# Rows of inverse norms by a ones-times-diagonal product, and state products in halves of 256 columns

## The chip, the cores and the metric

The kernel runs on one core of a Trainium2 chip. The metric is the device time of one execution in microseconds. Three runs of the kernel before took 3521.5, 3522.03 and 3524.02 us; their median, 3522.03 us, is the number to be changed. A measurement of this kernel can tell about 0.2% (7 us) from no change.

## What is computed

One layer of a hybrid model on 256 tokens behind 16 meta tokens (272 rows, width 2048, float32):

1. `n = rmsnorm(h)`, and one input projection `n @ w_in` for everything that follows.
2. A retention mixer with 8 heads: rotary on q and k, scores with a decay mask, values of 512 channels a head, then an RMS norm of each token over the 512 channels of its head, `o = _rms(o)`, times `silu(g)`, and an output projection of 4096 x 2048.
3. A state-space mixer with 8 groups of 8 heads of 64 channels: a causal convolution of width 4, a chunked scan over two chunks of 128 tokens (products within a chunk, and a state carried between chunks), times `silu(z)`, an RMS norm of each token over the 512 channels of its group, and a projection of 4096 x 2048.
4. Both mixers gated and added, projected, added to `h`; then an RMS norm over 2048 channels, a product-key selection of 16 of 16384 experts for each of 8 heads, and the experts' two layers (all 16384 rows of `peer_u` and `peer_v` are streamed), a last residual and norm.

There are thus 17 norms whose inverse must stand as a row over tokens, the same on every partition: 8 heads, 8 groups, and the norm ahead of the experts. Channels lie on the partitions and tokens along the free axis, so the sum over channels is a sum over partitions, and its result has to reach all partitions again.

## The kernel before

`Stream` (L35) fixes the order of all work. TensorE's main work is a queue of 2244 weight pieces of [128, 512]. Every piece is loaded by SyncE (L89, two pieces in one transfer of 512 KB), split on ScalarE into a rounded part `wh` (L99) and on VectorE into the rest `wl` (L100), and used by 12 float32r products (L202 to L204, four contraction tiles with three products each). The splits are written two pieces ahead of the products (`LEAD = 2`) and go through four buffers; loads are written six pieces ahead. All engines run their instructions strictly in the order in which they are written.

Everything else is written between the pieces by generators: `yield 3` means that the next step is written three pieces later, at the earliest; further numbers in a yield are microseconds of VectorE and ScalarE work, and such a step is put off to a later piece while credit for that engine is used up. So the order of instructions is fixed when the program is built and does not depend on times.

The retention part runs head after head, 48 pieces each (`ret_head`, steps `attend`, `gtile`, `gated`). Then come the retention's output projection, 8 state-space groups of 40 pieces (`ssm_group`, steps `btile`, `ctile`, `mats`, `xtile`, `scan`, `ztile`, `gated`), the second output projection (`mixer_out`, first 20 pieces of gates, then products that need the 32 tiles `Q.gh`/`Q.gl`), the residual (`resid`), the queries (`query`, `topk`), and the experts.

A norm is made by `norm_col` (L165): two products with a column of ones put the sums of 256 tokens into two PSUM columns (L169), one piece later VectorE (L162) and GpSimd (L163, a power of -0.5) make the inverse root `ncol`, 128 x 2. `to_rows` (L175) then writes it to DRAM with a transfer of 256 single elements (L178) and reads it back to all 128 partitions with a second (L179), both on GpSimd's queue; the second waits for the first in GpSimd's own order.

Who uses the row `r`: in `gated` of a head, VectorE's L367 (sg times r), then L369, ScalarE's L371 and VectorE's L373. In `gated` of a group, GpSimd's L699 (y times r, four pieces after the transfers are written), then ScalarE's L704 (gh) and VectorE's L708 (gl). In the residual, `Q.rb`, used by the experts.

In the state-space part GpSimd also carries, in this order between one group's norm and the next: `meta` (L610, a copy of the leading tokens), L620, the two products m times cb (L587), L638, transfers L597 and L554, L558, y times z (L687), and the sums of squares L691 and L692. The `meta` copy is what TensorE's L622 transposes, in the middle of the stream of pieces.

The two state products of `scan` (L631 and L633) are float32 products of 512 columns:

```python
z1 = P.pso.tile([128, 512], F32, name="sc")
pe.matmul(z1, bk0, x0.rearrange("p e s c -> p (e s c)"), start=True, stop=True)
z2 = P.pso.tile([128, 512], F32, name="tp", bufs=2)
pe.matmul(z2, bk, x1.rearrange("p h e -> p (h e)"), start=True, stop=True)
```

Of the kernel before, what the change touches and what calls it, by code (L numbers as in the profile page):

```python
# [34 lines left out]
class Stream:  # L35
    """The tensor engine's main work in order: weight pieces of [128, 512], each split into two float32r
    parts ahead of its products. Other work runs between the pieces, as generators. They yield the number of
    pieces to wait for and, where it is worth counting, how long the next step holds VectorE and ScalarE, in
    microseconds: a step that isn't urgent waits for a piece with time to spare."""
# [38 lines left out]
    def need(self, ready):  # L78
        """Emits the pending other work early until ready()."""
        while not ready():  # L80
            _, patient, _, gen, _ = heapq.heappop(self.side)
            self.step(gen, not patient, 0)
# [44 lines left out]
def build(ctx, tc, a):  # L127
# [32 lines left out]
    def rsqrt(dst, ps, mul, add):  # L160
        """dst = (mul * ps + add) ** -0.5"""
# [3 lines left out]
    def norm_col(w, psp, name, sq, mul, add):  # L165
        """Sums over the partitions of sq [128, S], as (mul * sum + add) ** -0.5 in [token, block]."""
# [6 lines left out]
        return c  # L173

    def to_rows(dst, c):  # L175
        """dst[p, t] for every partition p from [token, block]"""
        d = P.dram.tile([2, 128], F32, name="rows", bufs=4)
        pool.dma_start(d.rearrange("b t -> t b"), c)  # L178
        pool.dma_start(dst, bass.AP(tensor=d.tensor, offset=d.offset, ap=[[0, 128], [1, S]]))  # L179
# [5 lines left out]
    def product(srcs, moving, done, hook=None, count=None):  # L185
        """One output tile [128, n]: pieces of 4 contraction tiles, three float32r products for each.
        done(psum) is a generator with the rest; count() tells how many tiles of the moving operand are there."""
# [35 lines left out]
    # ------------------------------------------------------------ retention  # L223
    def ret_head(h):
# [76 lines left out]
        def attend():  # L301
# [43 lines left out]
            c = yield from norm_col(w, P.pso, "s0", sq[:, 0], 4.0 / 512, 4.0 * EPS)  # L345
            B["r"] = r = w.tile([128, S], F32, name="r")
            to_rows(r, c)
# [43 lines left out]
    # ------------------------------------------------------------ the mixers' output projections  # L391
# [37 lines left out]
    # ------------------------------------------------------------ state space  # L429
# [101 lines left out]
    def bc(x, n):  # L531
        """[p, 8] as [p, 8, n]"""
        return x.unsqueeze(2).to_broadcast([x.shape[0], 8, n])

    def ssm_group(g):
# [69 lines left out]
        def scan():  # L605
# [25 lines left out]
            pe.matmul(z1, bk0, x0.rearrange("p e s c -> p (e s c)"), start=True, stop=True)  # L631
            z2 = P.pso.tile([128, 512], F32, name="tp", bufs=2)
            pe.matmul(z2, bk, x1.rearrange("p h e -> p (h e)"), start=True, stop=True)  # L633
# [50 lines left out]
        def gated():  # L684
# [9 lines left out]
            c = yield from norm_col(P.ssm, P.pso, "s0", z[:, 0], 1.0 / 512, 4.0 * EPS)  # L694
            r = P.ssm.tile([128, S], F32, name="r")
            to_rows(r, c)
            yield 4
# [27 lines left out]
    # ------------------------------------------------------------ residual, expert queries  # L725
# [14 lines left out]
    def resid(j):  # L740
        def done(p):
# [16 lines left out]
            if j == NK - 1:  # L758
                yield 2
                Q.rt = yield from norm_col(P.bconst, P.psm, "mix", Q.ssq, 1.0 / D, EPS)  # L760
                to_rows(Q.rb, Q.rt)
                st.spawn(topk(), 1)
# [52 lines left out]
    def topk():  # L815
# [4 lines left out]
        def picked(b, h, pos, ixf):  # L820
            """The two key numbers of each of the 16 chosen pairs."""
# [66 lines left out]
    # ------------------------------------------------------------ experts  # L888
# [12 lines left out]
    def zblk(i, j, t0, t1):  # L901
        """Z[:, i:j, t0:t1] in at most two views with their start"""
# [150 lines left out]
    # ------------------------------------------------------------ the program  # L1053
# [211 lines left out]
```

## Time and profile before

| what | value |
|---|---|
| median of three runs | 3522.03 us |
| span of the profiled execution, first to last instruction | 3535.0 us |
| time of the profiled execution beside that span | not given by the page; the span alone is 13.0 us over the median |
| TensorE busy | 97% of the span |
| VectorE, ScalarE, GpSimd busy | 67%, 49%, 19% |
| mean granted TensorE clock | 0.984 |

A float32 product stands in the trace as two instructions (two passes), a float32r product as one. "Busy" counts an instruction from its start to its modelled end, and products overlap, so the sum over a line can be larger than the time that it takes; the idle time before an instruction, in brackets with what ended it, is the number used below. A piece of 256 columns takes 1.42 us, one of 272 columns 1.52 us.

### The profile page before, as it was taken

What the parts mean: (1) busy time and instruction counts of PE and PEld (TensorE: products, weight loads), DVE (VectorE), ACT (ScalarE), POOL (GpSimd) and SP (SyncE); (2) the same over time, 40 slices, a digit from 0 to 9 for tenths busy, and PEclk for the clock granted to TensorE, in tenths of its full rate; (3) what the DMA queues carried; (4) which work ended last, traced back from release to release, by engine and by line L of the source; (5) the groups of instructions that cost most, each with busy time, mean ns of one, the idle gap of its engine ahead of it and who ended that gap; (6) DMA issues with size and microseconds to landing.
All of it is one profiled execution on the core that took longest, in us unless ns stands there. A gap on an engine that the chain in (4) does not pass through costs nothing.

```text
span 3535.0 us, 66214 instructions
## 1 busy us (share of the span) xinstructions
PE 3414.0 (97%) x25242; PEld 3259.7 (92%) x25242; DVE 2352.7 (67%) x4550; ACT 1732.7 (49%) x3131; POOL 675.8 (19%) x784
## 2 busy tenths in 40 slices
PE   9999999999999998898999999999999999999999
PEld 8999989999998888888999999999999988888887
DVE  7555455555576776775556789989999755555555
ACT  5444444444454444444444555555555554555555
POOL 2111111100012222321002111156678500000000
PEclk9999999999999999999999999999999999999999
DMA  5566665566556565555556755655555566666665
GB/s 184 156 149 148 160 158 147 152 195 195 185 171 163 157 158 157 151 157 152 185 185 215 205 180 186 186 178 174 175 178 174 180 197 200 192 192 196 193 194 184
DMA packets 177613, 622.39 MB, mean 176 GB/s; under 512 B 21200, under 2 KB 27216, under 8 KB 177040
## 3 DMA queue, kind: packets, MB, share of 16 engines
q1 hardware_dynamic: 172288, 603.20, 58.0%
q0 software_dynamic: 5008, 14.96, 1.6%
q8 instruction: 198, 3.24, 0.4%
q14 instruction: 119, 0.97, 0.1%
HBM read 613.75 MB, written 4.34 MB: 175 GB/s over the span
## 4 chain that ended last, share of the span: by engine, by line
PE 86%; DMA 6%; issue 4%; POOL 2%; DVE 1%; ACT 1%; DVEq 0%; POOLq 0%; SPq 0%; ACTq 0%
PE acc L202 21%; PE acc L204 21%; PE acc L203 21%; PE y L1001 7%; PE y L1003 7%; PE y L1002 7%; DMA rows<-ncol 4%; DMA r<-rows 2%; PE g L933 1%; DVE wl L100 1%; POOL y L699 1%; PE yd L664 0%; POOL y L687 0%; POOL ncol L163 0%; PE sc L268 0%
## 5 line engine op out<-in xcount | busy, mean ns | idle before, releaser
L100 DVE TENSOR_TENSOR wl<-raw,wh 128x512 fp32r<-128x512 f32 x2244 | 1631.8, 731 | 1061.9 <-ACT wh L99 1043.4
L99 ACT ACTIVATE wh<-raw 128x512 fp32r<-128x512 f32 x2244 | 1407.1, 630 | 1341.2 <-PE acc L203 918.9
L204 PE MATMUL acc<-xh,wl 128*128 128x256 f32 (+1 forms) x3216 | 930.8, 289 | 38.3 <-DVE wl L100 38.1
L202 PE MATMUL acc<-xh,wh 128*128 128x256 f32 (+1 forms) x3216 | 943.3, 293 | 3.1 <-ACT wh L99 3.1
L203 PE MATMUL acc<-xl,wh 128*128 128x256 f32 (+1 forms) x3216 | 926.8, 288 | 0.0
L204 PEld LDWEIGHTS acc<-xh,wl 128*128 128x128 f32 x3216 | 620.2, 193 | 42.3 <-DVE wl L100 42.1
L204 PE MATMUL acc<-xgh,wl 128*128 128x256 f32 x2304 | 644.4, 280 | 0.0
L202 PE MATMUL acc<-xgh,wh 128*128 128x256 f32 x2304 | 643.9, 279 | 0.0
L203 PE MATMUL acc<-xgl,wh 128*128 128x256 f32 x2304 | 643.9, 279 | 0.0
L202 PEld LDWEIGHTS acc<-xh,wh 128*128 128x128 f32 x3216 | 621.1, 193 | 10.4 <-ACT wh L99 4.9
L203 PEld LDWEIGHTS acc<-xl,wh 128*128 128x128 f32 x3216 | 619.1, 193 | 1.9 <-issue 1.9
L203 PEld LDWEIGHTS acc<-xgl,wh 128*128 128x128 f32 x2304 | 432.8, 188 | 0.0
L204 PEld LDWEIGHTS acc<-xgh,wl 128*128 128x128 f32 x2304 | 432.5, 188 | 0.0
L202 PEld LDWEIGHTS acc<-xgh,wh 128*128 128x128 f32 x2304 | 432.3, 188 | 0.0
L1001 PE MATMUL y<-wh,wzh 128*128 128x512 f32 x1024 | 400.2, 391 | 0.0
L1003 PE MATMUL y<-wh,wzl 128*128 128x512 f32 x1024 | 398.7, 389 | 0.0
L1002 PE MATMUL y<-wl,wzh 128*128 128x512 f32 x1024 | 398.6, 389 | 0.0
L202 PE MATMUL acc<-gh,wh 128*128 128x256 f32 (+1 forms) x1152 | 330.2, 287 | 13.5 <-ACT wh L99 13.5
L203 PE MATMUL acc<-gl,wh 128*128 128x256 f32 (+1 forms) x1152 | 331.2, 288 | 2.0 <-DVE gl L708 1.9
L204 PE MATMUL acc<-gh,wl 128*128 128x256 f32 (+1 forms) x1152 | 330.0, 286 | 1.4 <-DVE wl L100 1.4
L202 PEld LDWEIGHTS acc<-gh,wh 128*128 128x128 f32 x1152 | 223.3, 194 | 14.1 <-ACT wh L99 13.7
L1003 PEld LDWEIGHTS y<-wh,wzl 128*128 128x128 f32 x1024 | 192.2, 188 | 40.2
(292 smaller groups left out, 3629.0 us busy)
## 6 DMA issues: line engine op xcount, KB each, us to landing
raw<-in_win SPq DMA_DIRECT2D x418, 512.0 KB, 3.6
raw<-in_pu SPq DMA_DIRECT2D x256, 512.0 KB, 3.5
raw<-in_pv SPq DMA_DIRECT2D x256, 512.0 KB, 3.5
raw<-in_wro SPq DMA_DIRECT2D x64, 512.0 KB, 3.5
raw<-in_wso SPq DMA_DIRECT2D x64, 512.0 KB, 3.5
raw<-in_wout SPq DMA_DIRECT2D x32, 512.0 KB, 4.0
raw<-in_wq SPq DMA_DIRECT2D x32, 512.0 KB, 3.7
m<-acs_d POOLq DMA_DIRECT2D x16, 512.0 KB, 7.1
```

The lines of the kernel that those rows point to most:

```text
L99: self.nc.scalar.activation(h, r, AF.Copy)
L100: self.nc.vector.tensor_sub(lo, r, h.bitcast(F32))
L202: pe.matmul(p, h[:, s], mh[:, kk], start=kk == 0, stop=False)
L203: pe.matmul(p, h[:, s], ml[:, kk], start=False, stop=False)
L204: pe.matmul(p, lo[:, s], mh[:, kk], start=False, stop=kk == nk - 1)
L699: pool.tensor_mul(y, y, r.unsqueeze(1).to_broadcast([128, 4, S]))
L933: pe.matmul(ps[:, t % NB].rearrange("p a b -> p (a b)"), o[:, 0], o[:, 1:].rearrange("p a b -> p (a b)"), start=True, stop=True)
L1001: pe.matmul(y, wh[:, s], h, start=i == 0, stop=False)
L1002: pe.matmul(y, wh[:, s], lo, start=False, stop=False)
L1003: pe.matmul(y, wl[:, s], h, start=False, stop=i == NE - 1)
```

## The change

A generator `norm_rows` takes the place of `norm_col` and `to_rows`. After the inverse root, GpSimd multiplies the identity with it: `diag`, 128 x 256, holds two diagonal matrices side by side. Three pieces later TensorE multiplies ones (128 x 128) with `diag`; the result, in the upper half of the PSUM tile that held the sums, is the row on every partition. One piece after that the generator returns. The heads use the row from PSUM; the groups and the residual copy it to SBUF on ScalarE. In the groups, the y times r step is then written one piece later than before. The two state products become four, of 256 columns each.

```diff
-    def norm_col(w, psp, name, sq, mul, add):
+    def norm_rows(w, psp, name, sq, diag, mul, add):
         ps = psp.tile([128, 512], F32, name=name)
         for b in range(2):
             pe.matmul(ps[:, b:b + 1], sq[:, b * 128:b * 128 + 128], ones[:, :1], start=True, stop=True)
         yield 1
         c = w.tile([128, 2], F32, name="ncol", bufs=2)
         rsqrt(c, ps[:, :2], mul, add)
-        return c
-
-    def to_rows(dst, c):
-        d = P.dram.tile([2, 128], F32, name="rows", bufs=4)
-        pool.dma_start(d.rearrange("b t -> t b"), c)
-        pool.dma_start(dst, bass.AP(tensor=d.tensor, offset=d.offset, ap=[[0, 128], [1, S]]))
+        pool.tensor_tensor(diag.rearrange("p (b t) -> p b t", b=2), ident.unsqueeze(1).to_broadcast([128, 2, 128]),
+                           c.unsqueeze(2).to_broadcast([128, 2, 128]), op=OP.mult)
+        yield 3
+        pe.matmul(ps[:, S:], ones, diag, start=True, stop=True)
+        yield 1
+        return c, ps[:, S:]
...
-            c = yield from norm_col(w, P.pso, "s0", sq[:, 0], 4.0 / 512, 4.0 * EPS)
-            B["r"] = r = w.tile([128, S], F32, name="r")
-            to_rows(r, c)
+            _, B["r"] = yield from norm_rows(w, P.pso, "s0", sq[:, 0], sq[:, 1], 4.0 / 512, 4.0 * EPS)
...
-            pe.matmul(z1, bk0, x0.rearrange("p e s c -> p (e s c)"), start=True, stop=True)
+            for i in (0, 256):
+                pe.matmul(z1[:, i:i + 256], bk0, x0.rearrange("p e s c -> p (e s c)")[:, i:i + 256],
+                          start=True, stop=True)
...
-            pe.matmul(z2, bk, x1.rearrange("p h e -> p (h e)"), start=True, stop=True)
+            for i in (0, 256):
+                pe.matmul(z2[:, i:i + 256], bk, x1.rearrange("p h e -> p (h e)")[:, i:i + 256],
+                          start=True, stop=True)
...
-            c = yield from norm_col(P.ssm, P.pso, "s0", z[:, 0], 1.0 / 512, 4.0 * EPS)
+            _, rp = yield from norm_rows(P.ssm, P.pso, "s0", z[:, 0], z[:, 1], 1.0 / 512, 4.0 * EPS)
             r = P.ssm.tile([128, S], F32, name="r")
-            to_rows(r, c)
-            yield 4
+            act.activation(r, rp, AF.Copy)
+            yield 1
...
-                Q.rt = yield from norm_col(P.bconst, P.psm, "mix", Q.ssq, 1.0 / D, EPS)
-                to_rows(Q.rb, Q.rt)
+                Q.rt, rp = yield from norm_rows(P.bconst, P.psm, "mix", Q.ssq, P.h2p.tile([128, S], F32, name="hsq", bufs=2), 1.0 / D, EPS)
+                act.activation(Q.rb, rp, AF.Copy)
```

## Rows read from the trace of the kernel before

**Rows 1.** The page: the span, the busy times of the engines, and the chain that ended last, by engine and by line (shares of the span).

```profile
span 3535.0 us, 66214 instructions
PE 3414.0 (97%) x25242; PEld 3259.7 (92%) x25242; DVE 2352.7 (67%) x4550; ACT 1732.7 (49%) x3131; POOL 675.8 (19%) x784
...
PE 86%; DMA 6%; issue 4%; POOL 2%; DVE 1%; ACT 1%; DVEq 0%; POOLq 0%; SPq 0%; ACTq 0%
```

**Rows 2.** Busy time by stage. Columns: the window's length, then busy time and (x instructions) of PE, weight loads, DVE, ACT and POOL, the granted clock, DMA share, GB/s. The stages are the heads, the first group (no norm of an earlier group falls in it), and the other groups with the start of the second output projection.

```profile
30.00:703.00 673.00, 635.28 (x4995) 626.07 (x4994) 358.92 (x588) 288.79 (x508) 76.03 (x91) 0.97 0.59 154
...
1005.00:1085.00 80.00, 79.49 (x648) 77.28 (x648) 61.20 (x121) 41.03 (x74) 17.85 (x15) 1.00 0.57 178
1085.00:1655.00 570.00, 504.36 (x3993) 486.56 (x3992) 388.20 (x706) 257.07 (x472) 145.11 (x116) 0.94 0.59 154
```

**Rows 3.** Groups of instructions by line, TensorE alone, in the window of the heads (30 to 703 us): busy time and mean, then idle time before them and what ended it.

```profile
L202 PE MATMUL acc<-xh,wh 128*128 128x256 f32 (+1 forms) x1437 | 421.4, 293 | 3.1 <-ACT wh L99 3.1
L204 PE MATMUL acc<-xh,wl 128*128 128x256 f32 (+1 forms) x1437 | 417.9, 291 | 34.3 <-DVE wl L100 34.3
```

**Rows 4.** The same view in the window of the groups and the start of the second output projection (1005 to 1655 us).

```profile
L204 PE MATMUL acc<-xh,wl 128*128 128x272 f32 (+1 forms) x1306 | 379.0, 290 | 4.0 <-DVE wl L100 3.8
L202 PE MATMUL acc<-gh,wh 128*128 128x256 f32 x54 | 16.0, 296 | 7.2 <-ACT wh L99 7.2
L203 PE MATMUL acc<-gl,wh 128*128 128x256 f32 x53 | 15.8, 298 | 1.9 <-DVE gl L708 1.9
L622 PE MATMUL tp<-ident,meta 128*64 128x128 f32 x8 | 3.2, 399 | 53.1 <-POOL meta L610 45.3 <-DVE xd L617 7.8
```

**Rows 5.** The timeline of the first head's norm: start and duration in us, engine, line, operation; in brackets the idle time before it and what ended that.

```profile
88.45 0.50 PE L169 MATMUL s<-ones,sq 128*128 128x1 f32 x4
91.06 0.94 POOL L178 DMA_DIRECT2D rows<-ncol  x1 [0.31 <-POOL ncol L163]
104.97 1.15 ACT L99 ACTIVATE wh<-raw 128x512 fp32r<-128x512 f32 x2 [5.25 <-DMA raw<-in_win]
108.43 1.23 DVE L367 TENSOR_TENSOR sg<-sg,r 128x1024 f32<-128x1024 f32 x1 [7.98 <-DMA r<-rows]
110.31 0.41 PE L204 MATMUL acc<-xh,wl 128*128 128x272 f32 x1 [4.14 <-DVE wl L100]
```

**Rows 6.** Transfers: KB of each and median us to landing; first those of the whole span, then the weights in the window 84 to 112 us.

```profile
raw<-in_win SPq DMA_DIRECT2D x418, 512.0 KB, 3.6
...
rows<-ncol POOLq DMA_DIRECT2D x17, 1.0 KB, 9.8
...
raw<-in_win SPq DMA_DIRECT2D x6, 512.0 KB, 11.0
```

**Rows 7.** The timeline around the norm of the second group, columns as in rows 5. The third row begins the last of the 16 contraction tiles of the four pieces that follow the sums; the product added by the change stands behind that tile.

```profile
1156.62 0.50 PE L169 MATMUL s<-ones,sz 128*128 128x1 f32 x4
1162.65 0.77 POOL L178 DMA_DIRECT2D rows<-ncol  x1 [0.30 <-POOL ncol L163]
1162.88 0.28 PE L202 MATMUL acc<-xh,wh 128*128 128x256 f32 x1
...
1182.13 0.23 POOL L610 COPY meta<-xs 128x64 f32<-128x64 f32 x1
1182.20 0.91 ACT L704 ACTIVATE gh<-y,gss 128x256 fp32r<-128x256 f32 x2 [8.17 <-POOL y L699]
1182.41 0.42 PE L622 MATMUL tp<-ident,meta 128*64 128x128 f32 x1 [8.20 <-POOL meta L610]
```

**Rows 8.** Busy time (columns of rows 2) in 16 windows, each from TensorE's first product after one of the 16 waits to the end of the half-clock stretch that the wait set off (clock 0.50 in 15 of them, 0.53 in the first): the sum of all.

```profile
sum 69.16, PE 67.28 PEld 66.96 DVE 51.77 ACT 44.95 POOL 9.32; mean PE 4.20 PEld 4.19 DVE 3.24 ACT 2.81 POOL 0.58
```

**Rows 9.** Starts of every third product of a piece, inside the last of these stretches and after it (timeline, TensorE).

```profile
1641.83 0.41 PE L202 MATMUL acc<-xh,wh 128*128 128x256 f32 x1
1642.47 0.41 PE L202 MATMUL acc<-xh,wh 128*128 128x256 f32 x1
...
1644.20 0.28 PE L202 MATMUL acc<-xh,wh 128*128 128x256 f32 x1
1644.56 0.28 PE L202 MATMUL acc<-xh,wh 128*128 128x256 f32 x1
```

**Rows 10.** The nearest operations to those added. First the chain in order of time (start us, us on the chain, what): L268 is four passes of 256 and four of 144 columns, L631 two passes of 512. Then groups by line: a product of 256 elements a partition with an operand spread by a zero step on GpSimd, and an activation of 256 elements out of PSUM on ScalarE.

```profile
130.74 1.35 PE sc L268 x8
1034.74 1.05 PE sc L631 x2
...
L829 POOL TENSOR_TENSOR oh<-oh,ixf 128x256 f32<-128x256 f32 x32 | 32.1, 1021 | 43.1 <-DVE oh L827 43.1
L677 ACT ACTIVATE cth<-acc 128x256 f32<-128x256 f32 x32 | 12.2, 380 | 33.6 <-PE acc L204 32.2 <-issue 1.4
```

**Rows 11.** GpSimd beside VectorE and TensorE (timeline): the m times cb products of the fifth interval, and y times z of the third.

```profile
1419.58 5.20 POOL L587 TENSOR_TENSOR m<-m,cb 128x1024 f32<-128x1024 f32 x2 [3.52 <-ACT m L584]
1422.46 2.87 DVE L100 TENSOR_TENSOR wl<-raw,wh 128x512 fp32r<-128x512 f32 x1
1425.39 0.39 PE L204 MATMUL acc<-xh,wl 128*128 128x256 f32 x1 [1.42 <-DVE wl L100]
...
1225.74 2.40 POOL L687 TENSOR_TENSOR y<-y,sz 128x1024 f32<-128x1024 f32 x1 [2.64 <-DVE y L669]
1226.61 2.08 DVE L100 TENSOR_TENSOR wl<-raw,wh 128x512 fp32r<-128x512 f32 x1 [0.95 <-ACT wh L99]
```

## The prediction

> **What bounds the kernel now.** I read the chain first, then the busy times by stage, then what TensorE waits for, line by line, and last the timeline of one wait of each kind. TensorE is busy for 97% of the 3535.0 us span, and the chain runs through it for 86%; what is left on the chain is mostly DMA, 6%, a great deal for a kernel whose weights stream ahead of their use [rows 1]. The stages show where. The first state-space group, in which no earlier norm falls, runs at full clock with TensorE idle for 80.00 - 79.49 = 0.51 us. The heads leave it idle for 673.00 - 635.28 = 37.7 us at a mean clock of 0.97, the later groups with the start of the second output projection for 570.00 - 504.36 = 65.6 us at 0.94 [rows 2]. So TensorE is the bound, and whatever it waits for in these two stages is paid in full.
>
> In the heads all of it but 0.3 us stands ahead of two lines: 34.3 us for `wl` and 3.1 us for `wh`, 37.4 us in 8 heads [rows 3]. The timeline of the first shows why: the inverse root leaves GpSimd at 91.06, its two transfers end only at 108.43, and VectorE, which is to multiply with the row, stands idle for 7.98 us with the next `wl` behind it, until TensorE has used up what was split ahead and waits 4.14 us [rows 5]. In the groups, L622 waits 53.1 us in 7 places [rows 4]: GpSimd stands in y times r until the row lands, ScalarE waits 8.17 us in gh behind it, and the small `meta` copy, which TensorE's transpose needs, is queued behind y times r; TensorE waits 8.20 us [rows 7]. At the second output projection the last group's row is late too: 7.2 us for `wh` behind a blocked gh and 1.9 us for gl [rows 4].
>
> Each wait is paid twice. After each of the 16, the granted clock stands at its lower level, 1.2 GHz: TensorE was busy for 67.3 us in such stretches [rows 8]. There three products start every 0.64 us, and 0.36 us at 2.4 GHz [rows 9], so 67.3 x (1 - 0.36/0.64) = 29.4 us were lost.
>
> **The change part by part.**
>
> *Transfers removed.* The waits worth 37.4 + 53.1 + 7.2 + 1.9 = 99.6 us end with them, and with the waits the slow stretches, 29.4 us: 129.0 us. What is late next in a head: the sums start at 88.45 and the root is ready at 91.06 [rows 5], the diagonal some 1.1 us later, at 92.2; TensorE comes to the added product after the sums (0.4 us) and four pieces of 1.42 us, at 94.5, and need not wait. VectorE reaches L367 at about 100.5, so the row has 5 us to spare. Nothing else that it needs is late, because the weight load that ScalarE awaited for 5.25 us was itself slowed while the 256 single elements were written: loads landed after 11.0 us there against a median of 3.6 [rows 5, 6].
>
> *Product added.* 17 products of ones with 256 float32 columns, two passes each. Four passes of 256 columns and four of 144 take 1.35 us [rows 10]: 0.84 ns a column, so 0.22 us a pass and 0.43 a product; 0.02 more for the change of weights gives 17 x 0.45 = 7.7 us, all on the path (from 17 x 0.3, if passes overlap with neighbours, 5 us, to 17 x 0.6, 10 us).
>
> *A new wait, TensorE for the diagonal.* TensorE runs in order, so all later pieces queue behind this product, and the two split buffers fill behind them. In a group the sums start at 1156.62 and the root is free at 1162.65; TensorE comes to the product at 1162.88 + 0.36 = 1163.24 [rows 7]. GpSimd's multiply is not in the trace; a 256-element product with a spread operand took 1.02 us [rows 10], so the diagonal stands at 1163.7 to 1163.8 and TensorE waits some 0.55 us in each of six groups: 3.3 us. The first and last groups and the residual have their root sooner. The bounds are 0 (root sooner when nothing is blocked) and 2 us in each of the 8 groups, 16 us (VectorE, which makes the root, later by another 1.5 us).
>
> *ScalarE's copy*, 9 times 0.38 us [rows 10], comes when the split that ScalarE does next still has no free buffer; I cost it at nothing. Without that cover it is 9 x 0.4 = 3.6 us.
>
> *y times r, gh and gl one piece later.* GpSimd now starts y times r some 8.5 us after the sums, so that gh could follow at 11 us; before, gh started 1182.20 - 1156.62 = 25.6 us after them [rows 7]. The `meta` copy, by the yields three pieces behind y times r, finds GpSimd free. For gh and gl every group but the last has the 40 pieces of another group as room. The last has not: its last gl was written just ahead of the piece that reads it, and now follows by one step; I count 0.7 us, between 0 and 2.
>
> *The port that VectorE and GpSimd share.* Now y times r ran while VectorE was stopped anyway; after the change it runs beside the splits, and the diagonal multiply is new. In the trace a `wl` took 2.87 us while GpSimd made m times cb for 5.20 us, and TensorE then waited 1.42 us; beside y times z another took 2.08 us and TensorE did not wait [rows 11]. All such waits in the groups are 3.8 us now [rows 4], some of them covered because TensorE had just run at half clock. Without that cover I put m times cb at 1.2 us in each of seven groups, 8.4 us, which is 5 us more than now; 0 to 20 us are possible. The Trainium skill, SBUF — State Buffer, section "SBUF: two separate sides", states that a VectorE operation with two SBUF inputs and a GpSimd operation that reads SBUF exclude each other for a whole instruction. By that rule, which speaks against this change, 17 diagonals and 8 times y times r could block VectorE for 17 x 1.0 + 8 x 2.3 = 35 us, and none of it need reach TensorE while splits lie ahead; the 2.87 us and 2.08 us above agree with it.
>
> *Halves of 256 columns.* A pass of 512 columns takes 1.05 / 2 = 0.525 us where two of 256 at the rate above take 0.43 [rows 10]. 32 such passes give 32 x 0.1 = 3.2 us. If the rate belongs to the operands and not to the width, it is 0; twice as many weight loads could cost 1 us.
>
> *The sum.* Against the profiled span: 129.0 + 3.2 - 7.7 - 3.3 - 0.7 - 5 = 115.5 us, from 3535.0 to 3419.5. The median lies 13.0 us under that span. I put these 13 us into work that stays and take the same gain off the median: 3522.0 - 115.5 = 3406.5 us.
>
> **Rivals.**
>
> *The profile's surplus lies in the waits.* If the 13.0 us by which the profiled span is longer are transfers slowed by the recording, the unrecorded kernel has less to win: 102.5 us, 3419.5. For it speaks that the experts' stage has no waits at which recording could cost time; against it, that 13 us over 16 waits of 4 to 8 us would be a large part of each.
>
> *VectorE becomes the bound in the groups.* It is busy for 61.2 of 80.0 us in the first group [rows 2], where gh and gl are still missing, and the groups get shorter. If the root comes 1.5 us later and port locks cost TensorE 3 us a group in place of 1.2, that is 8 x 1.5 + 7 x 1.8 = 25 us more: 3431. For it speaks the 6 us from sums to root [rows 7] against 2.6 in a head [rows 5].
>
> *The weight loads stay late in the heads*, because something else slows them: without the row's wait the next `wl` could still not start before 105.6, and TensorE would wait about 0.5 to 1 us in each of 8 heads, 8 us at most: 3414. Against it: 11.0 us of landing falls together with the element-wise transfer [rows 6].
>
> *Slower than before: TensorE parked behind the diagonal.* GpSimd's multiply, with both operands spread by zero steps, could take x us where I count 1.0. TensorE would then wait x - 0.6 in six groups and about x - 3.2 in the other 11 places, with a slow stretch of 29.4 / 16 = 1.8 us after each. Without any such wait the gain is 118.8 us; 17x - 38.8 + 31 reaches it at x = 7.4 us. At x = 9 the time would be 3522 + 26 = 3548. Against it stands a product with one spread operand at 1.02 us [rows 10]; no row shows two.
>
> That the change does not do what it says I see in the halves alone: 3410.
>
> **How the numbers follow.** My forecast, with its own range of 3396 to 3416 (halves and the product's price at either end, locks 0 to 10 us): 0.60. VectorE as the bound, 3431: 0.18. Surplus in the waits, 3419: 0.12. Late loads, 3414: 0.05. Parked, 3548: 0.03. A gain under 7 us by a mixture that I cannot name: 0.02. The range, 3394 to 3433, takes in the surplus, the late loads and most of the VectorE case. About 0.2%, 7 us, can be told from no change: faster 0.95, the same 0.02, slower 0.03.
>
> **What would show it.** The profile after should have no wait of more than 1.5 us in the heads, and L622 should wait for nothing. The mean clock should be near 1.00 from 30 us on. L169's successor should show some 0.5 us of waiting for the diagonal in groups 2 to 7, none in heads. Passes of 256 columns should follow each other every 0.22 us. `raw` loads should land after 3 to 5 us everywhere. I would be wrong if waits for `wl` in the groups exceeded 15 us, if the clock fell again behind waits for the diagonal, or if the diagonal's multiply took over 3 us.

## The result, and the profile after

The changed kernel takes 3401.99 us (median of four runs, 3401.59 to 3403.01) where the kernel before, with one more run beside the three, takes 3522.2 (3521.5 to 3524.02). The ratio is 0.9657, 95% interval 0.9646 to 0.9669. The gain of 120.2 us stands against 115.5 in the sum, the time against a predicted 3406.5.

The page of the changed kernel, span, busy times and chain by engine, answers to [rows 1]:

```profile
span 3400.4 us, 66296 instructions
PE 3382.4 (99%) x25308; PEld 3240.5 (95%) x25308; DVE 2359.6 (69%) x4550; ACT 1738.2 (51%) x3140; POOL 667.4 (20%) x767
...
PE 99%; DVE 0%; issue 0%; ACT 0%; DMA 0%; POOL 0%; SPq 0%; DVEq 0%; POOLq 0%
```

DMA, 6% of the chain before, is gone from it, and TensorE is busy for 99% of the span. The busy times by stage answer to [rows 2], with the same windows:

```profile
30.00:703.00 673.00, 672.75 (x5466) 666.80 (x5465) 388.94 (x631) 316.53 (x551) 70.22 (x83) 1.00 0.54 168
1005.00:1085.00 80.00, 80.00 (x668) 78.19 (x665) 63.05 (x116) 41.17 (x77) 25.26 (x20) 1.00 0.59 185
1085.00:1655.00 570.00, 570.00 (x4721) 562.06 (x4719) 424.32 (x749) 297.28 (x539) 124.84 (x96) 1.00 0.58 178
```

TensorE's idle time in the first and the third falls from 37.7 and 65.6 us to 0.25 and 0, and the clock stands at 1.00, the level of 2.4 GHz, in all three. The groups by line from 25 to 2100 us answer to [rows 3, 4]; the waits of L204 and L202 (now L205 and L203), 34.3 and 3.1 us in the heads alone, are 0.5 and 0, and the 53.1 us ahead of the transpose of `meta` (now L621) are 0. The two added products, L178, waited for nothing in all 16 heads and groups:

```profile
L203 PE MATMUL acc<-xh,wh 128*128 128x256 f32 (+1 forms) x3216 | 930.4, 289 | 0.0
L205 PE MATMUL acc<-xh,wl 128*128 128x256 f32 (+1 forms) x3216 | 915.6, 285 | 0.5 <-DVE wl L100 0.5
...
L178 PE MATMUL s<-sz,ones 128*128 128x256 f32 x16 | 4.8, 379 | 0.0
L178 PE MATMUL s<-sq,ones 128*128 128x256 f32 x16 | 4.7, 378 | 0.0
L621 PE MATMUL tp<-ident,meta 128*64 128x128 f32 x8 | 2.2, 270 | 0.0
```

Where the time came from can be read from the products of the sums, one set in each norm, which both kernels have at the same place in the order (32 instructions in 8 heads, 32 in 8 groups, 4 at the residual; durations in ns, then the first and the last start). Before:

```profile
L169 PE MATMUL s<-ones,sq x32: 164/250/251, 88.4 to 678.0; 128*128 128x1 f32 x32
L169 PE MATMUL s<-ones,sz x32: 165/250/251, 1077.7 to 1612.2; 128*128 128x1 f32 x32
L169 PE MATMUL mix<-ones,ssq x4: 167/250/251, 1975.7 to 1975.9; 128*128 128x1 f32 x4
```

After:

```profile
L171 PE MATMUL s<-ones,sq x32: 164/250/251, 88.5 to 631.0; 128*128 128x1 f32 x32
L171 PE MATMUL s<-ones,sz x32: 165/250/251, 1022.9 to 1485.4; 128*128 128x1 f32 x32
L171 PE MATMUL mix<-ones,ssq x4: 166/250/251, 1839.9 to 1840.1; 128*128 128x1 f32 x4
```

From the first head's sums to the last head's it was 589.6 us and is 542.5; from there to the first group's 399.7 and 391.9; through the groups 534.5 and 462.5; to the residual's 363.5 and 354.5; from there to the end of the span 1559.3 and 1560.5. So the heads gave 47.1 + 7.8 = 54.9 us, the groups 72.0 and the rest 9.0 - 1.2 = 7.8, together 134.7 between the two profiled executions.

The timeline around the first head's norm (start, duration, line; in brackets the idle time before it and what ended it) answers to [rows 5]:

```profile
88.49 0.50 PE L171 MATMUL s<-ones,sq 128*128 128x1 f32 x4
90.08 0.72 POOL L163 TENSOR_TENSOR ncol<-ncol,mhalf 128x2 f32<-128x2 f32 x1 [5.14 <-DVE ncol L162]
90.87 0.61 POOL L175 TENSOR_TENSOR sq<-ident,ncol 128x256 f32<-128x256 f32 x1
94.62 0.59 PE L178 MATMUL s<-sq,ones 128*128 128x256 f32 x2
100.82 1.21 DVE L366 TENSOR_TENSOR sg<-sg,s 128x1024 f32<-128x1024 f32 x1
```

The diagonal is ready at 91.48, 3.1 us before TensorE comes to it, and VectorE's product with the row starts at 100.82 instead of 108.43 and waits for nothing. Around the second group's norm, which answers to [rows 7], the diagonal is ready at 1096.48, 0.6 us before TensorE comes to it:

```profile
1090.72 0.50 PE L171 MATMUL s<-ones,sz 128*128 128x1 f32 x4
1094.49 1.10 POOL L163 TENSOR_TENSOR ncol<-ncol,mhalf 128x2 f32<-128x2 f32 x1 [4.72 <-DVE ncol L162]
1095.67 0.81 POOL L175 TENSOR_TENSOR sz<-ident,ncol 128x256 f32<-128x256 f32 x1
1097.10 0.59 PE L178 MATMUL s<-sz,ones 128*128 128x256 f32 x2
1098.19 2.42 POOL L702 TENSOR_TENSOR y<-y,r 128x1024 f32<-128x1024 f32 x1 [1.71 <-ACT r L699]
```

The weight loads in the window 84 to 112 us (KB of each, median us to landing) answer to the last line of [rows 6], 11.0 us before:

```profile
raw<-in_win SPq DMA_DIRECT2D x9, 512.0 KB, 3.8
```

### The profile page after: what moved, and what is told of

Read it like the earlier page. It is cut to its first block, busy times and chain, and to the rows that moved or that the text cites. A ratio compares the mean times of both kernels' runs of the same rounds, so it can differ in the third digit from the quotient of the medians.

```text
span 3400.4 us, 66296 instructions
## 1 busy us (share of the span) xinstructions
PE 3382.4 (99%) x25308; PEld 3240.5 (95%) x25308; DVE 2359.6 (69%) x4550; ACT 1738.2 (51%) x3140; POOL 667.4 (20%) x767
## 4 chain that ended last, share of the span: by engine, by line
PE 99%; DVE 0%; issue 0%; ACT 0%; DMA 0%; POOL 0%; SPq 0%; DVEq 0%; POOLq 0%
PE acc L203 25%; PE acc L205 25%; PE acc L204 24%; PE y L1004 7%; PE y L1006 7%; PE y L1005 7%; PE g L936 1%; PE yd L667 1%; PE sc L269 0%; PE tp L635 0%; PE sc L631 0%; PE o L333 0%; PE tp L653 0%; PE mix L798 0%; PE y L1033 0%; PE tp L651 0%
## 5 line engine op out<-in xcount | busy, mean ns | idle before, releaser
L203 PE MATMUL acc<-xh,wh 128*128 128x256 f32 (+1 forms) x3216 | 930.4, 289 | 0.0
L205 PE MATMUL acc<-xh,wl 128*128 128x256 f32 (+1 forms) x3216 | 915.6, 285 | 0.5 <-DVE wl L100 0.5
L204 PE MATMUL acc<-xl,wh 128*128 128x256 f32 (+1 forms) x3216 | 913.6, 284 | 0.0
L205 PE MATMUL acc<-xgh,wl 128*128 128x256 f32 x2304 | 645.1, 280 | 0.0
L203 PE MATMUL acc<-xgh,wh 128*128 128x256 f32 x2304 | 643.8, 279 | 0.0
L204 PE MATMUL acc<-xgl,wh 128*128 128x256 f32 x2304 | 643.3, 279 | 0.0
L203 PEld LDWEIGHTS acc<-xh,wh 128*128 128x128 f32 x3216 | 606.5, 189 | 4.2 <-issue 1.4
L205 PEld LDWEIGHTS acc<-xh,wl 128*128 128x128 f32 x3216 | 606.4, 189 | 0.7 <-DVE wl L100 0.7
L204 PEld LDWEIGHTS acc<-xl,wh 128*128 128x128 f32 x3216 | 605.7, 188 | 0.6
L204 PEld LDWEIGHTS acc<-xgl,wh 128*128 128x128 f32 x2304 | 433.0, 188 | 0.0
L205 PEld LDWEIGHTS acc<-xgh,wl 128*128 128x128 f32 x2304 | 432.8, 188 | 0.0
L203 PEld LDWEIGHTS acc<-xgh,wh 128*128 128x128 f32 x2304 | 431.5, 187 | 0.0
L203 PE MATMUL acc<-gh,wh 128*128 128x256 f32 (+1 forms) x1152 | 329.6, 286 | 6.4 <-ACT wh L99 6.4
L205 PE MATMUL acc<-gh,wl 128*128 128x256 f32 (+1 forms) x1152 | 329.5, 286 | 1.1 <-DVE wl L100 1.0
L204 PE MATMUL acc<-gl,wh 128*128 128x256 f32 (+1 forms) x1152 | 330.5, 287 | 0.1
L1005 PEld LDWEIGHTS y<-wl,wzh 128*128 128x128 f32 x1024 | 192.4, 188 | 39.3
```

The costliest lines, as they stand in the source:

```text
L203: pe.matmul(p, h[:, s], mh[:, kk], start=kk == 0, stop=False)
L204: pe.matmul(p, h[:, s], ml[:, kk], start=False, stop=False)
L205: pe.matmul(p, lo[:, s], mh[:, kk], start=False, stop=kk == nk - 1)
L1005: pe.matmul(y, wh[:, s], lo, start=False, stop=False)
```

## The experiments

The theory is the prediction's: each of 17 norms made engines wait for a row that took two transfers, TensorE paid these waits and then a stretch at 1.2 GHz, and the product through TensorE costs little as long as the diagonal is ready when TensorE comes. Open were five things: where the surplus of the profiled execution lies; whether the late weight loads were a cause of their own; what the halves and the place of the product are worth; whether a late diagonal would cost as much as argued; and whether the diagonal is needed at all. The edits stand against the changed kernel. Each run was compared with the kernel before on the same chip; that kernel took 3546.79 to 3549.32 us (medians) there, on four chips, against 3522 in the first measurement.

**The kernel before, once more.**

> The kernel before, unchanged, to see whether its runs spread as its profile did. The profile of before had a span of 3535.0 us, 13.0 us over the median of its runs; the profile after has a span of 3400.4, 1.6 us under its median. Theory (the surplus lay in the waits for transfers, whose length changes from one execution to the next): a span about 1.7 us under the time of its run, near 3520, in which the waits of VectorE for r in the heads and of TensorE at the transpose of meta are together 10 to 15 us shorter than the 37.4 + 53.1 us of the first profile. Rival (the recording makes every run with transfers longer by the same amount, outside the waits): a span of 3535 again, 13 us over its time, with the waits at 90 us.

It took 3548.16 us (3543.45 to 3549.97, 10 runs). The span of its profiled execution was 3545.1 against a time of 3546.92: a span is 1.8 us under its run's own time, as the theory had it, so the recording did not make this execution longer. But the span did not come near 3520, and the waits were in sum not shorter but longer than in [rows 3, 4]: on these three lines 100.2 us, against 3.1 + 34.3 + 4.0 + 53.1 = 94.5:

```profile
L202 PE MATMUL acc<-xh,wh 128*128 128x256 f32 (+1 forms) x3216 | 945.1, 294 | 7.5 <-ACT wh L99 7.5
L204 PE MATMUL acc<-xh,wl 128*128 128x256 f32 (+1 forms) x3216 | 932.2, 290 | 35.2 <-DVE wl L100 35.0
...
L622 PE MATMUL tp<-ident,meta 128*64 128x128 f32 x8 | 3.2, 400 | 57.5 <-POOL meta L610 49.4 <-DVE xd L617 8.1
```

The write of the row landed after a median of 10.8 us here, 9.8 in [rows 6]. This span is 10.1 us longer than that of [rows 1], and all of it but 0.1 us lies ahead of the residual's sums, from which on both take 1559.3 and 1559.4 us:

```profile
L169 PE MATMUL mix<-ones,ssq x4: 166/250/250, 1985.7 to 1985.9; 128*128 128x1 f32 x4
```

So between these two profiled executions the time of the kernel before moves with its transfers and the waits for them. That the same holds between 3522 us in the first measurement and 3547 in the later ones is likely but not shown, since no execution of 3522 us was profiled. The changed kernel, and its version with 512 columns below, took 3401.59 to 3403.31 us in the first measurement and in a later one.

**A write that nobody reads.** The transfer of 256 single elements is put back into the changed kernel; nothing waits for it and nothing else is changed.

```diff
         pool.tensor_tensor(diag.rearrange("p (b t) -> p b t", b=2), ...
+        pool.dma_start(P.dram.tile([2, 128], F32, name="rows", bufs=4).rearrange("b t -> t b"), c)
         yield 3
```

> The changed kernel, with the 256 single elements of the inverse root written to DRAM as before the change, 17 times, and nobody reading them. Theory (loads that land late are covered by the six pieces by which they are written ahead): raw loads beside the write land after 7 to 12 us, ScalarE waits for some of them, TensorE for less than 0.5 us a time: 3402 to 3406 us. Rival (late loads were a part of the waits of before): TensorE waits 0.5 to 2 us in each of 17 places, 3411 to 3436 us.

3447.87 us (3441.18 to 3458.74): 45.9 us more than the changed kernel, 2.7 us in each of 17 places. In the window 88 to 112 us the weight loads land late again:

```profile
raw<-in_win SPq DMA_DIRECT2D x6, 512.0 KB, 9.2
...
rows<-ncol POOLq DMA_DIRECT2D x1, 1.0 KB, 11.1
```

ScalarE's timeline shows the stop of [rows 5], 5.25 us then, though no row is awaited any more:

```profile
105.17 1.15 ACT L99 ACTIVATE wh<-raw 128x512 fp32r<-128x512 f32 x2 [5.00 <-DMA raw<-in_win]
```

Over the whole kernel (the view of who waited for whom: total us, times, longest) ScalarE stood 73.6 us in 16 places for weights, and what hangs on its splits reached TensorE, most of it at the transpose of `meta`, behind VectorE:

```profile
ACT wh L99 <- DMA raw<-in_win: 73.6, 16, 6.4
...
PE tp L622 <- DVE xd L617: 17.4, 7, 3.9
```

In the changed kernel the first line is this, and the second is absent:

```profile
ACT wh L99 <- DMA raw<-in_win: 0.8, 1, 0.8
```

So the late loads, which the prediction read as a consequence that would go with the write, are a cost by themselves in this kernel. The kernel before took 144.8 us more on this chip than the changed one in the first measurement (3546.79 - 3401.99; its version with 512 columns took 3402.46 here). The write alone accounts for 45.9 us; if the costs simply add up, some 99 are left for the wait for the row and its read. That they add up is not shown: in the kernel before the late loads and the wait for the row fall into the same microseconds.

**What about the write is slow.** Four more unread writes at the same place: 128 pieces of 1 KB; 128 pieces of 8 bytes that adjoin; 256 pieces of 4 bytes with gaps of 4 bytes; 128 pieces of 4 bytes that adjoin.

```diff
+        pool.dma_start(P.dram.tile([128, S], F32, name="rows", bufs=4), sq)
+        pool.dma_start(P.dram.tile([128, 2], F32, name="rows", bufs=4), c)
+        pool.dma_start(P.dram.tile([128, 2, 2], F32, name="rows", bufs=4)[:, :, 0], c)
+        pool.dma_start(P.dram.tile([128, 1], F32, name="rows", bufs=4), c[:, :1])
```

> The changed kernel with an unread write from GpSimd's queue at the place of the one that cost 46 us, but of 128 pieces of 1 KB (the squares' tile) in place of 256 single elements of 4 bytes: 128 times the bytes. Theory (what slows the weight loads is the number of single elements, not a write as such): weight loads land after 3 to 5 us, no wait of TensorE, 3402 to 3405 us. Rival (any write between the loads delays them): waits as with the element-wise write, 3430 us or more.

> The unread write again, now as 128 pieces of 8 bytes (each partition's two values side by side) in place of 256 of 4 bytes. The write of 256 single elements cost 46 us in 17 places, 2.7 us each; that of 128 pieces of 1 KB cost nothing. Theory (each small piece holds a transfer engine for a time of its own, so the number of small pieces decides): about half, 3418 to 3428 us. Rival (only pieces of a single element are slow): 3402 to 3406 us. A third way (the six pieces of loads ahead cover half the delay entirely): 3402 to 3410 us, with weight loads in that window still landing after 6 us or more, which would tell it from the second.

> The unread write of each norm has again 256 pieces of 4 bytes, but in the order of the tokens and with a gap of 4 bytes between them, where e4's pieces were written in transposed order, every second one 512 bytes away. Theory: the pieces of 4 bytes, 256 of them, are what holds up the loads, whatever their order: as e4, 3440 to 3455 us, the write lands after 9 us or more. Rival: the transposed order in DRAM did it: 3402 us, the write lands after 3 to 5 us.

> The unread write of each norm is one column: 128 pieces of 4 bytes, next to each other. Theory (each piece of 4 bytes costs time): half of e4's price, 1.35 us in each of 17 places, 3425 us (3415 to 3435). Rival (the number of pieces or their order decides, not their size: 128 pieces of 8 bytes cost nothing): 3402 us.

| unread write | lands after (median, us) | `raw`, 88 to 112 us (median) | `raw` issued from 90 to 93 us | time (us) |
|---|---|---|---|---|
| none (the changed kernel) | | 3.8 | 4.3 | 3401.99 |
| 128 x 1 KB | 2.1 to 4.1 by its place | 3.9 | 4.1 | 3402.06 (3401.59 to 3402.13) |
| 128 x 8 bytes, adjoining | 4.8 | 4.2 | 6.9 | 3401.70 (3401.19 to 3401.89) |
| 256 x 4 bytes, gaps | 5.2 | 4.3 | 7.4 | 3402.09 (3401.44 to 3402.90) |
| 128 x 4 bytes, adjoining | 9.1 | 7.6 | 12.1 | 3428.27 (3426.26 to 3429.55) |
| 256 x 4 bytes, two adjoining runs of 128 (before's) | 10.3 | 9.2 | 12.9 | 3447.87 (3441.18 to 3458.74) |

The fourth column is the one load issued just beside the first head's write, which the median over the window hides; beside the second head's write it is 7.4 us with 8 bytes and 7.8 with gaps. The windows right behind the first write (columns as in [rows 2]; the last number is GB/s) show the same. The changed kernel:

```profile
95.00:98.00 3.00, 3.00 (x26) 2.97 (x26) 1.11 (x2) 1.23 (x3) 0.00 (x0) 1.00 0.78 246
```

With gaps:

```profile
95.00:98.00 3.00, 3.00 (x26) 2.97 (x26) 1.13 (x2) 1.22 (x3) 0.00 (x0) 1.00 0.45 35
98.00:103.00 5.00, 5.00 (x42) 5.00 (x42) 3.95 (x7) 2.34 (x4) 0.00 (x0) 1.00 0.88 311
```

Adjoining, 128 x 4 bytes:

```profile
95.00:98.00 3.00, 3.00 (x25) 2.95 (x25) 0.79 (x2) 1.54 (x3) 0.00 (x0) 1.00 0.53 30
98.00:103.00 5.00, 5.00 (x42) 5.00 (x41) 3.44 (x5) 1.26 (x2) 0.00 (x0) 1.00 0.60 30
```

From 95 to 98 us all four forms with pieces of 4 or 8 bytes hold the transfers of this core down, to 67 GB/s or less, where the changed kernel moves 246 and the one with pieces of 1 KB 256. With 8 bytes and with gaps the stop is over by 98 us; with the adjoining 4 bytes it goes on to 103, at 24 to 30 GB/s. The shorter stop costs no time: a load that lands after 6.9 or 7.4 us still comes early enough, and ScalarE waits for weights for 0.7 and 3.3 us in the whole kernel. With the longer one it waits 44.0 us (one column) and 73.6 us. This is the third way that the text on the 8 bytes named: the loads written ahead cover a delay of half the length. The column costs 57% of the two runs (26.3 us against 45.9). The theory on the gaps fell as far as the time goes, and so did the rival's transposed order, since one column in plain order costs 1.5 us a time.

The Trainium skill, DMA: Bandwidth & Descriptors, section "Specifications", gives 512 bytes as the least transfer for full rate, with a read-modify-write below it. These runs go with it as far as pieces of 1 KB held nothing up and all the smaller ones did; it does not part the 4 bytes with gaps from those that adjoin. Why the adjoining ones hold the loads up about twice as long is open.

**The row through DRAM again, used later.** The heads and seven groups write the row to DRAM, read it seven pieces later and use it five pieces after that; the last group and the residual keep the product.

```diff
+    def late_rows(w, psp, name, sq, dst, mul, add):
...
+        pool.dma_start(d.rearrange("b t -> t b"), c)
+        yield 7
+        pool.dma_start(dst, bass.AP(tensor=d.tensor, offset=d.offset, ap=[[0, 128], [1, S]]))
+        yield 5
```

> The changed kernel, but in the 8 heads and the first 7 groups the row goes through DRAM again, with the transfers written apart and used late: the write one piece after the sums, the read 7 pieces later, the use 5 pieces after that. The last group and the residual keep the product of ones and diagonal. Theory (only the waiting for the transfers cost time, not the transfers): no wait of TensorE in heads and groups, and 15 x 0.43 = 6.4 us less TensorE work: 3395.5 us. Rival (the element-wise write slows the weight loads, which landed after 11.0 us in the profile of before, and TensorE waits for them): 0.5 to 1 us in each of 15 places on top, 3403 to 3411 us, with ScalarE waiting some 5 us for raw in each head.

3434.54 us (3429.78 to 3438.31), 32.5 above the changed kernel. TensorE's waits, 25 to 2100 us:

```profile
L217 PE MATMUL acc<-xh,wh 128*128 128x256 f32 (+1 forms) x3216 | 928.5, 289 | 6.1 <-ACT wh L99 6.1
L219 PE MATMUL acc<-xh,wl 128*128 128x256 f32 (+1 forms) x3216 | 920.6, 286 | 8.5 <-DVE wl L100 8.0
...
L635 PE MATMUL tp<-ident,meta 128*64 128x128 f32 x8 | 2.2, 275 | 10.0 <-DVE xd L630 9.4 <-POOL meta L623 0.6
```

More distance alone brings most of the gain, 112 of 145 us, but not all. What is missing is about what the write alone would cost: 2.7 us for each of 15 writes, less the 0.43 us of each product saved, is an estimate of 34 us against the measured 32.5. GpSimd still stood 24.0 us in all before y times r in six groups, so this run does not part the write from the wait as cleanly as the unread write does; of TensorE's 10.0 us at the transpose only 0.6 was GpSimd's.

**512 columns again.**

```diff
-            for i in (0, 256):
-                pe.matmul(z1[:, i:i + 256], bk0, ...[:, i:i + 256], start=True, stop=True)
+            pe.matmul(z1, bk0, x0.rearrange("p e s c -> p (e s c)"), start=True, stop=True)
```

(and z2 likewise)

> The changed kernel with the two state products of a group as 512 columns again. The traces show 1.05 us for two passes of 512 and 1.06 us for four of 256. Theory (the extra 0.1 us of each pass that I ascribed to the width belongs to the start of the product and stays): 3402 us, within 1 us of the changed kernel. Rival (the prediction's: halves save 0.1 us in each of 32 passes): 3405 us.

3402.46 us (3401.79 to 3403.31): the halves are worth nothing that can be told apart. The chain through the first group of the changed kernel (start, us on the chain, what) says why:

```profile
979.94 1.06 PE sc L631 x4
981.00 1.06 PE tp L635 x4
```

With 512 columns it reads so:

```profile
980.73 1.05 PE sc L630 x2
981.78 1.06 PE tp L632 x2
```

Four passes of 256 take as long as two of 512. In the timeline the four end 0.22 us apart, which is the rate that I took from [rows 10] and 0.87 us for all; some 0.19 us of the product lies at its ends, at either width. I had divided 1.05 us by two passes, and so charged these 0.19 us to the width.

**The product one or two pieces after the diagonal, not three.**

```diff
-        yield 3
+        yield 1
         pe.matmul(ps[:, S:], ones, diag, start=True, stop=True)
-        yield 1
+        yield 3
```

and the same with `yield 2` in both places.

> The changed kernel with the product of ones and diagonal written one piece after the diagonal in place of three, and the two pieces put behind it, so that the use of the row stays where it was. In the profile after, the diagonal is ready 3.0 us after the sums begin in a head and 5.8 in a group; TensorE would now come to the product after 3.2 and some 3.35 us. Theory (a wait of TensorE in its own order is paid in full, a short one without a fall of the clock): no wait in heads, 2.4 us in seven groups: 3402 + 17 to 20 = 3419 to 3422 us, clock 0.999. Rival (the time is made up, since splits run on during the wait): 3402 to 3405 us.

> The changed kernel with the product two pieces after the diagonal in place of three, and one piece put behind it. With one piece ahead TensorE waited 2.17 us in seven groups, six of them with a half-clock stretch, and the kernel took 27.6 us more. At two pieces TensorE comes some 4.9 us after the sums, the diagonal stands after 5.8 to 5.9. Theory (a wait under 1 us is paid alone, the clock holds): 7 x 0.9 to 1.1 us: 3408 to 3410 us, clock 0.999. Rival (any wait behind the other float32 products there sets off a half-clock stretch): 3418 us or more, clock 0.996.

One piece: 3429.57 us (3428.59 to 3430.24), 27.6 more, above the range that I gave. TensorE waited 2.17 us in each of seven groups, 15.2 in all, and in no head:

```profile
1028.87 1.22 PE L178 MATMUL s<-sz,ones 128*128 128x256 f32 x2 [2.17 <-POOL sz L175]
```

Just behind it (windows, columns as in [rows 2]) the clock stands at 0.50, the level of 1.2 GHz, and a microsecond later at 1.00, 2.4 GHz; it fell like this behind six of the seven waits:

```profile
1030.00:1032.00 2.00, 2.00 (x11) 2.00 (x10) 0.00 (x0) 0.00 (x0) 0.00 (x0) 0.50 0.20 74
1033.00:1036.00 3.00, 3.00 (x28) 3.00 (x27) 2.16 (x5) 2.27 (x5) 1.08 (x1) 1.00 0.17 15
```

Two pieces: 3410.00 us (3409.56 to 3410.39), 8.0 more; seven waits of 0.67 us, 4.7 in all, and the clock stays at 1.00 behind them:

```profile
1029.73 0.70 PE L178 MATMUL s<-sz,ones 128*128 128x256 f32 x2 [0.67 <-POOL sz L175]
...
1030.00:1034.00 4.00, 4.00 (x34) 3.95 (x34) 3.21 (x7) 1.73 (x4) 1.26 (x1) 1.00 0.64 233
```

Three pieces are the least that cost nothing here.

**TensorE parked behind the diagonal.** The multiply of the diagonal is written twelve times.

```diff
-        pool.tensor_tensor(diag.rearrange(...
+        for _ in range(12):
+            pool.tensor_tensor(diag.rearrange(...
```

> The changed kernel with GpSimd making each diagonal 12 times over, to park TensorE behind it: the prediction's rival on the other side, made real. 11 more of 0.61 us in a head and 0.81 us in a group put the diagonal at 9.7 and 14.7 us after the sums, where TensorE comes after 6.1 and 6.4: waits of 3.6 us in ten places and 8.3 us in seven, 94 us. Theory (a wait of 3 us or more costs its length and a stretch at half clock, 1.8 us on average): 94 + 31 = 125 us, 3527 us, 17 half-clock stretches. Rival (the lost clock of before belonged to the transfers' waits, in which all engines stood): no fall of the clock, 3496 us.

3555.86 us (3555.03 to 3557.12), against 3549.32 before on this chip: ratio 1.002, 1.0011 to 1.0029. That is more than the 3527 us expected, mainly since twelve multiplies took 9.80 us in the first head where I had counted 12 x 0.61. The clock fell behind all 17 waits, so the rival without a fall is out.

```profile
L179 PE MATMUL s<-sz,ones 128*128 128x256 f32 x16 | 9.8, 714 | 59.4 <-POOL sz L176 59.4
L179 PE MATMUL s<-sq,ones 128*128 128x256 f32 x16 | 9.8, 714 | 47.7 <-POOL sq L176 47.7
```

59.4 + 47.7, and 6.3 at the residual, are 113.4 us of waits; the time is 153.9 above the changed kernel, so that some 40 us, 2.4 a wait, came on top of the idle time that the trace counts. This is the rival that ends on the other side, made real, and its formula comes close: with x = 9.8 us, 17x - 38.8 + 31 gives 158.8 us. The whole gain hangs on a diagonal that is ready in time.

**Rows without a diagonal.** In heads and groups, ones times the squares puts the sums on all partitions at once; then the inverse root has 256 elements a partition instead of 2.

```diff
+    def direct_rows(psp, name, sq, dst, mul, add):
+        ps = psp.tile([128, 512], F32, name=name)
+        pe.matmul(ps[:, :S], ones, sq, start=True, stop=True)
+        yield 1
+        rsqrt(dst, ps[:, :S], mul, add)
```

> The changed kernel, but in heads and groups the sums come as rows at once: one product of ones (128 x 128) with the squares, 256 columns, in place of two products with a column of ones, a diagonal and the product with it; VectorE and GpSimd then make the inverse root of 128 x 256 in place of 128 x 2. The residual keeps the diagonal. Theory: TensorE loses 0.36 us in each of 16 places, 5.8 us: 3396 us, if GpSimd's power of 256 elements takes under some 8 us. Rival (GpSimd's power is slow per element: 0.72 us for 2, so up to 92 us for 256): waits of VectorE for r in heads and of TensorE at the transpose in groups, above 3450 us.

3931.68 us (3930.68 to 3940.29). GpSimd's power is why:

```profile
L163 POOL TENSOR_TENSOR sz<-sz,mhalf 128x256 f32<-128x256 f32 x8 | 331.8, 41481 | 53.2 <-DVE sz L162 53.2
L163 POOL TENSOR_TENSOR sq<-sq,mhalf 128x256 f32<-128x256 f32 x8 | 329.0, 41131 | 42.8 <-DVE sq L162 42.8
```

41.1 us for 256 elements a partition against 0.72 for 2 in the timeline above. The root on one column a token, and the diagonal, pay.

## Why the prediction was right, and where not

*Waits and clock.* Right in place. All 16 waits of [rows 3, 4] are gone, the clock is at 1.00 in heads and groups, and waits of 0.9 us for `wl` in two places and one of 0.2 us are all that TensorE's products have from 47 us on. The sum was low: by its terms the heads should give 37.4 + 8 x 29.4/16 - 8 x 0.45 = 48.5 us, the groups 57.3 (53.1 + 7 x 29.4/16 + 2.8 for the halves, less 7 x 0.45, less 3.3, less 5) and the rest 9.7; measured between the two profiled executions were 54.9, 72.0 and 7.8. That is 19.1 us more than 115.5.

*The steps that were mis-sized.* "TensorE waits some 0.55 us in each of six groups: 3.3 us" was 0: the root was ready sooner, and the diagonal took 0.81 us there and 0.61 in a head, not 1.02. The prediction had also read the start of the write, 0.30 us after GpSimd's power ended, as the end of the root [rows 5, 7]. The port, 5 us more than now in the sum, went the other way: the waits for `wl` in the groups, 3.8 us before, are 0. A pair of `wl` beside y times r took 2.27 us (1099.48) where two take 1.4, so GpSimd did hold VectorE up, and the splits lying ahead covered it. The Trainium skill, SBUF — State Buffer, section "SBUF: two separate sides", has such VectorE and GpSimd operations exclude each other; this trace agrees, and none of it reached TensorE. The 3.2 us for the halves of 256 columns were 0, and so were the 0.7 us for the last gl. The 0.45 us a product were 0.43 on the chain (94.78), 7.3 us in all. And each wait hid more than its idle time: a product counts as busy for 0.28 us, but the next would have started after 0.12, which is 16 x 0.16 = 2.6 us. These come to 3.3 + 8.8 - 3.2 + 0.7 + 0.4 + 2.6 = 12.6 of the 19.1 us; some 6.5 stay unassigned. They may belong to the waits too: with the product two pieces after the diagonal, seven waits cost 8.0 us and count as 4.7 us of idle time, 0.47 us hidden in each without any fall of the clock. At that rate, an estimate, 16 waits would hide 7.5 us and not 2.6; no run shows it for the kernel before.

*"I put these 13 us into work that stays."* This step failed, in the other direction. The gain of the two profiled executions is 134.6 us, of the medians 120.2. The changed kernel, and the four variants that cost nothing beside it, lie between 3401.19 and 3403.31 us on every chip used, their profiled executions among them (3400.4 us of span in 3402.12 us), while the kernel before lies between 3521.5 and 3558.65 by measurement and execution. So the surplus of the profiled execution of before lay in what the change removed. Longer transfers and waits are the likely reason, as between the two profiled executions of the kernel before. The rival "the profile's surplus lies in the waits" had the place right, and not the reason, since the recording added nothing when the kernel before was run again. Its 3419.5 missed because it rested on the same terms. That 3406.5 came within 4.5 us of the result is partly luck: two errors of 19 and 14 us had opposite signs.

*The other rivals.* VectorE did not become the bound: it is busy for 424.32 of 570.00 us in the groups, and the root was ready 1094.49 + 1.10 - 1090.72 = 4.9 us after the sums began, not 6. The late loads did end with the write, as [rows 5, 6] were read, so their rival fell; the unread write shows that they cost 45.9 us by themselves, which the prediction had as a side effect. Parked has its price confirmed; in the changed kernel the diagonal takes 0.61 to 0.81 us in heads and groups and 1.01 at the residual, and the rival does not come up.

*The marks named beforehand.* No wait in the heads, none at the transpose, the clock at 1.00 and loads that land after 3.8 us in the first head all came out as said. So did the passes every 0.22 us, though nothing hung on them. That loads land after 3 to 5 us "everywhere" did not, for single ones took up to 9.8. The 0.5 us behind the sums in the groups did not come.

## What to carry to other kernels

A value that has to change from partitions to the free axis can go through TensorE in 0.43 us, even where TensorE is the bound, if what it multiplies is ready before TensorE comes to it: with the product one piece after the diagonal the kernel took 27.6 us more here, with two pieces 8.0. A small transfer is priced not only by who waits for it but by what lands beside it; writing it without reading it, in the kernel that no longer needs it, measures that part alone. A median over many loads can hide the one that was held up, and a stop that the loads ahead just cover costs nothing until it gets longer. A profiled execution that lies above the median may owe it to its waits, and the kernel that waits for transfers took 25 us more in the later measurements while its successor without them took the same time in all.

## What was not expected of the hardware

- Small unread writes held up the weight loads of 512 KB beside them: the load issued beside the first head's write landed after 12.1 and 12.9 us with 128 and 256 elements of 4 bytes that adjoin in DRAM, after 7.4 us with 256 elements and gaps of 4 bytes, after 6.9 us with 128 pieces of 8 bytes, and after 4.1 us with 128 pieces of 1 KB (4.3 without a write). Only the first two cost time.
- TensorE's clock fell to 1.2 GHz behind six of seven idle times of 2.17 us and behind none of 0.67 us, in these places.
- GpSimd's power takes some 41.1 / 256 = 0.16 us per element of a partition; a product of 256 elements with both operands spread by zero steps took 0.61 to 1.01 us.
- A float32 state product took 1.05 us in two passes of 512 columns and 1.06 us in four of 256: 0.19 us of it does not depend on the columns.
